# A hybrid decoder trunk on one core: half-width down-weight sums, weights read straight from the input, sums beside the stored blocks, and longer runs ahead and at the end

## The chip, the core and the metric

The kernel runs on one core of a Trainium2 chip. The core has a matrix engine (TensorE, PE in the rows), a vector engine (VectorE, DVE), a scalar engine (ScalarE, ACT), GpSimd (POOL) and a sync engine (SyncE, SP) that issues nearly all transfers here. The metric is the device time of one execution in microseconds. The three runs of the kernel before took 1681.66, 1688.73 and 1690.01 us; their median is 1688.73 us.

## The reference

One decoder layer over 1024 tokens of width 1024: two attention branches, a mixed output product, a layer norm, a SwiGLU feed-forward of inner width 2816, and a second layer norm. The change touches only the feed-forward and what follows it.

```python
proj = x @ w_in[l]
o_a = _fox_attention(...)          # forgetting attention, 8 heads of 64
o_b = _dsa_attention(...)          # indexer, top-k keys, attention with ALiBi
merged = (sigmoid(g_a) * (o_a @ w_branch_a[l]) + sigmoid(g_b) * (o_b @ w_branch_b[l]))
x = _layer_norm(ALPHA * x + merged @ w_out[l], ln1_g[l], ln1_b[l])
gate, up = jnp.split(x @ w_ffn_in[l], 2, axis=-1)
ffn = (silu(gate) * up) @ w_ffn_out[l]
x = _layer_norm(ALPHA * x + ffn, ln2_g[l], ln2_b[l])
```

## The kernel before

Every product of matrices is made from three matmuls: each operand is split into a high part, rounded by ScalarE (`split`, line 770, for the up weights; line 898 for the last product), and a low part, the difference, made by GpSimd (lines 771 and 900) or VectorE (line 899); `mm3` multiplies high by high (line 99), low by high (100) and high by low (101).

Projections and attention fill the first half of the program. Then come the branch products, the output product and the first layer norm. The feed-forward is done by a seven-product scheme over two-by-two blocks of tokens, features and columns instead of eight plain products. Its up part runs over 22 chunks c of 128 inner columns. A chunk loads its gate weights (tag `wraw`, 2 buffers) and up weights (`wup`, 2 buffers). VectorE makes four sums r1 to r4 of them (lines 818 to 821), and the seven weight blocks are split into slots of a ring (`slot`). The seven products of 12 matmuls each follow in a fixed order: the two of `c11` (weights a11, a12), then s2, s3, s1, s4 and a22. VectorE takes each product out of PSUM with one or two additions (lines 787 and 838); ScalarE applies the gate's function; lines 846 and 847 finish the two halves of h. PSUM holds eight products at a time.

The order of TensorE's work is as the program is written. The streams of the other engines are each in order, too, but a scheduler chose that order when the kernel was built: it places a VectorE instruction of one chunk ahead of or behind those of another by its own estimate of when they become ready. An engine whose next instruction must wait holds back all that stand behind it.

Two chunks (`AHEAD`) have their `c11` done before the loop, between the transposes (`turn`) of the normalised tokens; the first two chunks of the loop then start with s2.

The down part needs, for each pair j of chunks, seven sums of blocks of h and seven sums of blocks of the down weights. Both are made inside the up loop and stored to DRAM, to `abd[p][j]`, p being the product. After each odd chunk, a buffer `wb` (one buffer of 128x2048) is loaded with the down weights of the pair; three of its four blocks are stored as they are (line 859); four sums are made in place by VectorE (lines 860 to 863) and stored (line 865). The blocks of h go the same way: three are stored plain (line 868), four sums are made in place over them (lines 869 to 872), and these are stored (line 874). A sum in place must wait until the store of the block that it overwrites is done.

The last part makes the seven down products in the order p = 1, 2, 6, 5, 3, 7, 4, each over 11 pairs j, and each j over four token tiles t of 3 matmuls. `prepare(p, j)` loads one `abd[p][j]` of 512 KB and splits it. The first seven loads use the two `wraw` buffers, later ones mostly `fraw` (4 buffers). `closing(p, t)` adds a product to the output rows. The last product, p = 4, runs its first five j over all four tiles in turn and then its last six (`LASTC`) tile by tile, so that each tile's layer norm can start while the next tile is multiplied. The first norm's result is read back (`y<-ydr`) during p = 2 and p = 6, at j = 4.

Of the kernel before, what the change touches and what calls it, by code (L numbers as in the profile page):

```python
# [8 lines left out]
F32 = mybir.dt.float32  # L9
F32R = mybir.dt.float32r  # L10
# [3 lines left out]
OP = mybir.AluOpType  # L14
# [21 lines left out]
IDX_SCALE = (8 ** -0.5) * (64 ** -0.5)  # L36

NMM, NT = 2, 2
AHEAD, LASTC, HURRY = 2, 6, 100
NG = (1, 1, 2, 2, 2, 2, 2, 4)  # L40
ORDER = (3, 0, 2, 1)
PHB, PLB = 3, 3
# [7 lines left out]
def trunk_kernel(ctx: ExitStack, tc: tile.TileContext, xT, xn, wt, wbr, wout, wfi, wfo,  # L50
                 lnp, bf, alq, alk, out):
    nc = tc.nc
    te, dve, act, pool, sp = nc.tensor, nc.vector, nc.scalar, nc.gpsimd, nc.sync
# [10 lines left out]
    wp, _w = open_pool("wp")  # L64
# [3 lines left out]
    def f(ap):  # L68
        return ap.bitcast(F32)
# [60 lines left out]
    abd = [[dram.tile([128, 2, 512], F32, name=f"abd{p}_{j}") for j in range(PAIRS)] for p in range(8)]  # L130
# [37 lines left out]
    z = idx.tile([128, L], F32, name="z", tag="t4", bufs=4)  # L168
    for h in range(2):
        s = slice(h * 512, h * 512 + 512)  # L170
        ps = ps_mm()
# [22 lines left out]
    u = t4("u")  # L194
# [27 lines left out]
    r2 = [idx.tile([128, L], F32R, name=f"r2{i}", tag="t4", bufs=4) for i in range(2)]  # L222
# [18 lines left out]
    for c in range(4):  # L241
        w = split_w(raw0, pool) if c == 0 else load_w(wt[C_IQ + c])
        iq = [idx.tile([128, 768], F32R, name="iq", tag="iq", bufs=4) for _ in range(2)]
        for q, (half, c0, n, d0) in enumerate(((0, 256, 256, 0), (1, 0, 512, 256))):
            ps = ps_mm()
# [6 lines left out]
        for a in range(2):  # L252
            h = 2 * c + a
            for i in range(2, 8):
                n = 128 * (i + 1)
# [477 lines left out]
    for t in range(NB):  # L733
        half, c0 = divmod(t * 128, 512)
        bs = fin.tile([128, 2, 6], F32, name="bs", tag="bs", bufs=2)
        for n in range(2):
            ns = slice(n * 512, n * 512 + 512)
            ps = ps_b()
# [54 lines left out]
    for c in range(AHEAD):  # L793
        raw = load_raw(wfi[c])
        w = [slot(), slot()]
# [9 lines left out]
        return psC.tile([128, 512], F32, name="pb", tag="pb", bufs=8)  # L805

    ffl, _ffl = open_pool("ffl")
    ring[0:0] = [(ffl, f"wt{k}", 1) for k in range(4)]
    for c in range(FC):
        g = load_raw(wfi[c])  # L810
        up = ffl.tile([128, 1024], F32, name="wup", tag="wup", bufs=2)
        sp.dma_start(up, wfi[FC + c])
        g1_, g2_, u1_, u2_ = g[:, 0:512], g[:, 512:1024], up[:, 0:512], up[:, 512:1024]
        new = c >= len(ahead)
        a11, a12 = (slot(), slot()) if new else (None, None)
        s2, s3, s1, s4, a22 = (slot() for _ in range(5))
        r1, r2, r3, r4 = (ffl.tile([128, 512], F32, name="ss", tag="ss", bufs=4) for _ in range(4))
        dve.tensor_tensor(r1, u1_, u2_, op=OP.add)
        dve.tensor_tensor(r2, r1, g1_, op=OP.subtract)
        dve.tensor_tensor(r3, g1_, u1_, op=OP.subtract)  # L820
        dve.tensor_tensor(r4, g2_, r2, op=OP.subtract)
        if new:
            split(a11, g1_)
            split(a12, g2_)
        split(s2, r2)
        split(s3, r3)
        split(s1, r1)
        split(s4, r4)
        split(a22, u2_)
        u = c11(ps_c, (a11, a12)) if new else ahead[c]  # L830
        h = ffl.tile([128, 2, 512], F32, name="h", tag="h", bufs=3)
        U, sg, h0, h1 = u[:, 0], u[:, 1], h[:, 0], h[:, 1]

        def add(to, w, x, *more):
            ps = ps_c()
            product(ps, w, x)
            for o, i in ((to, to), *more) if to is not None else more:
                dve.tensor_tensor(o, ps, i, op=OP.add)

        add(U, s2, T2)  # L840
        add(None, s3, T3, (h0, U))
        add(None, s1, T1, (h1, h0), (U, U))
        add(U, s4, B22)
        act.activation(U, U, AF.Silu)
        add(h0, a22, T4)
        dve.tensor_tensor(h1, h1, U, op=OP.mult)
        dve.tensor_tensor(h0, h0, sg, op=OP.mult)
        if c % 2 == 0:
            even = h
            continue  # L850


        j = c // 2
        wb = ffl.tile([128, 2, 1024], F32, name="wb", tag="wb", bufs=1)
        for x in range(2):
            sp.dma_start(wb[:, x], wfo[(c - 1 + x) * 128:(c + x) * 128])
        b11, b12, b21, b22 = wb[:, 0, 0:512], wb[:, 0, 512:1024], wb[:, 1, 0:512], wb[:, 1, 512:1024]
        for p, b in ((1, b11), (2, b21), (3, b22)):
            sp.dma_start(abd[p][j][:, 1], b)
        dve.tensor_tensor(b11, b12, b11, op=OP.subtract)  # L860
        dve.tensor_tensor(b12, b22, b12, op=OP.subtract)
        dve.tensor_tensor(b22, b22, b11, op=OP.subtract)  # L862
        dve.tensor_tensor(b21, b21, b22, op=OP.subtract)  # L863
        for p, b in ((5, b11), (7, b12), (6, b22), (4, b21)):
            sp.dma_start(abd[p][j][:, 1], b)
        a11, a21, a12, a22 = even[:, 0], even[:, 1], h0, h1
        for p, a in ((1, a11), (2, a12), (4, a22)):
            sp.dma_start(abd[p][j][:, 0], a)
        dve.tensor_tensor(a22, a21, a22, op=OP.add)
        dve.tensor_tensor(a21, a11, a21, op=OP.subtract)  # L870
        dve.tensor_tensor(a11, a22, a11, op=OP.subtract)
        dve.tensor_tensor(a12, a12, a11, op=OP.subtract)
        for p, a in ((5, a22), (7, a21), (6, a11), (3, a12)):
            sp.dma_start(abd[p][j][:, 0], a)
    _ffl.close()
    _ffr.close()
# [10 lines left out]
    def prepare(p, j):  # L887
        k = len(fring)
        fring.append(None)
        if k % 2 == 0:  # L890
            big = xm.tile([128, 2, 4, 512], F32R, name="fs", tag="x", bufs=4) if k // 2 % 6 < 4 else \
                fe.tile([128, 2, 4, 512], F32R, name="fs", tag="fs", bufs=2)
            fring[k] = big
        s = fring[k - k % 2][:, k % 2]
        raw = wp.tile([128, 1024], F32, name="wraw", tag="wraw", bufs=2) if k < 7 or k % 3 == 0 else \
            fe.tile([128, 1024], F32, name="fraw", tag="fraw", bufs=4)
        sp.dma_start(raw, abd[p][j].rearrange("p a n -> p (a n)"))
        act.activation(s[:, 0:2].rearrange("p a n -> p (a n)"), raw, AF.Copy)  # L898
        dve.tensor_tensor(s[:, 2], raw[:, 0:512], f(s[:, 0]), op=OP.subtract)  # L899
        pool.tensor_tensor(s[:, 3], raw[:, 512:1024], f(s[:, 1]), op=OP.subtract)  # L900
        return s[:, 0], s[:, 2], s[:, 1], s[:, 3]
# [10 lines left out]
    def scaled(o, i):  # L912
        dve.scalar_tensor_tensor(o, o, ALPHA, i, op0=OP.mult, op1=OP.add)

    def plus(o, ps, a=None):
        dve.tensor_tensor(o, ps, o if a is None else a, op=OP.add)

    def closing(p, t, ps):

        y, z = (yt + [None] * NB)[t:t + 5:4]  # L920
        u, bs, bz = us[t], bss[t], bss[t + 4]
        if p == 1:
            act.activation(u, ps, AF.Copy)
        elif p == 2:
            scaled(y[:, ha], ps)
            plus(y[:, ha], u)
            dve.bn_stats(bs[:, 0, :], y[:, ha])
        elif p == 6:
            plus(u, ps)
        elif p == 5:  # L930
            v = fy.tile([128, 512], F32, name="v", tag="v", bufs=2)
            plus(v, ps, u)
            scaled(y[:, hb], v)
            scaled(z[:, hb], v)
        elif p == 3:
            plus(y[:, hb], ps)
            dve.bn_stats(bs[:, 1, :], y[:, hb])
            for ns in layer_norm(fy, y, bs, *V2, True):
                sp.dma_start(out[t * 128:t * 128 + 128, ns], y[:, ns])
        elif p == 7:  # L940
            plus(u, ps)
            plus(z[:, hb], ps)
            dve.bn_stats(bz[:, 1, :], z[:, hb])
            scaled(z[:, ha], u)
        else:
            plus(z[:, ha], ps)
            dve.bn_stats(bz[:, 0, :], z[:, ha])
            for ns in layer_norm(fy, z, bz, *V2, t < 2):
                sp.dma_start(out[(t + 4) * 128:(t + 5) * 128, ns], z[:, ns])

    for p in (1, 2, 6, 5, 3, 7, 4):
        acc = [psD.tile([128, 512], F32, name="acc", tag="acc", bufs=8) for _ in range(4)]
        tiles = []
        for j in range(PAIRS):
            if j == 4 and p in (2, 6):
                for t in range(4):
                    yt.append(fy.tile([128, D], F32, name=f"y{len(yt)}"))
                    sp.dma_start(yt[-1], ydr[len(yt) - 1])
            elif j == 4 and p == 5:
                V2.extend((ln_vec(fy, 2), ln_vec(fy, 3)))  # L960
            if p == 1 and j < 5:
                with tc.high_priority(offset=HURRY):
                    tiles.append(prepare(p, j))
            else:
                tiles.append(prepare(p, j))
            if p != 4 or j < PAIRS - LASTC:
                for t in range(4):
                    step(acc, t, tiles[j:], j)
        for t in range(4):
            if p == 4:  # L970
                step(acc, t, tiles[PAIRS - LASTC:], PAIRS - LASTC)
            closing(p, t, acc[t])
# [59 lines left out]
```

## Time and profile before

| | value |
|---|---|
| median of three runs | 1688.73 us |
| the profiled execution, its own time | 1686.29 us |
| its span (first to last instruction) | 1684.4 us |
| TensorE matmuls, busy | 1606.5 us (95%) |
| VectorE busy | 1160.9 us (69%) |
| ScalarE busy | 771.7 us (46%) |
| GpSimd busy | 671.3 us (40%) |
| moved by DMA | 216.18 MB, 128 GB/s on average |

TensorE is busy nearly all the time, so the time is the sum of its matmuls and of the places where it stands still or runs at its lower clock. Such places are found by asking for the busy time of stretches of the span; what ended each stop is found by asking for the waits in that stretch. The up loop runs from 1026.8 to 1457.6 us of the span, the down products from 1457.6 to 1673.1 us.

### The profile page before, as it was taken

Reading aid. Unit: us, or ns where it says so; the run is one execution under the profiler, and the core shown is the slowest. Engines: PE = TensorE matmul, PEld = TensorE weight load, DVE = VectorE, ACT = ScalarE, POOL = GpSimd, SP = SyncE. Lnnn points to the kernel's source line nnn. Section 1 sums busy time; section 2 is a strip of 40 time slices with the busy share of each in tenths; the row PEclk is TensorE's granted clock in tenths of the full one; section 3 lists DMA queues with packets and bytes.
Section 4 is the critical chain, followed back from the end, with each engine's and each line's share of the span. In section 5 each row is a group of like instructions: output and inputs, shape, how many; then the busy total and the mean of one; then the engine's idle time right before and its main releaser. Section 6 shows DMA issues by size and latency. Waiting matters only on the chain. (4 is left out here: it accounts for less than half of the span.)

```text
span 1684.4 us, 22398 instructions
## 1 busy us (share of the span) xinstructions
PE 1606.5 (95%) x7722; PEld 1312.0 (78%) x7722; DVE 1160.9 (69%) x2016; ACT 771.7 (46%) x1368; POOL 671.3 (40%) x646
## 2 busy tenths in 40 slices
PE   7898999998999999999989998999899999999997
PEld 5776887776888888888767876887778888878885
DVE  6889999979645454544466668868786665557577
ACT  6777878884444444544322024222233323254341
POOL 1122333332333333333432036444455444377673
PEclk9999999999999999999999998999999999999998
DMA  5112212121222222223886115677643332497652
GB/s 176 47 40 65 60 45 59 57 70 43 57 68 61 70 57 74 59 63 124 272 257 242 77 51 175 233 247 257 234 160 120 106 107 93 143 342 272 190 165 93
DMA packets 83817, 216.18 MB, mean 128 GB/s; under 512 B 10164, under 2 KB 14260, under 8 KB 83704
## 3 DMA queue, kind: packets, MB, share of 16 engines
q1 hardware_dynamic: 83704, 214.75, 39.0%
q8 instruction: 61, 1.00, 0.2%
q14 instruction: 52, 0.43, 0.1%
HBM read 139.93 MB, written 65.87 MB: 122 GB/s over the span
## 5 line engine op out<-in xcount | busy, mean ns | idle before, releaser
L99 PE MATMUL mm<-xh,whi 128*128 128x512 f32 (+1 forms) x720 | 296.4, 412 | 15.5 <-ACT whi L146 6.4
L101 PE MATMUL mm<-xl,whi 128*128 128x512 f32 (+1 forms) x720 | 281.9, 392 | 1.2 <-DVE xl L156 1.2
L100 PE MATMUL mm<-xh,wlo 128*128 128x512 f32 (+1 forms) x720 | 281.4, 391 | 0.5 <-DVE wlo L147 0.5
L478 POOL TENSOR_SCALAR p<-p,st 128x512 f32<-128x512 f32 (+1 forms) x192 | 113.3, 598 | 321.3 <-DVE st L475 268.6
L93 POOL TENSOR_TENSOR wlo<-wraw,whi 128x1024 fp32r<-128x1024 f32 x51 | 123.1, 2414 | 192.3 <-ACT whi L92 171.0
L771 POOL TENSOR_TENSOR w<-ss,w 128x512 fp32r<-128x512 f32 x88 | 130.4, 1496 | 165.6 <-ACT w L770 158.2
L101 PEld LDWEIGHTS mm<-xl,whi 128*128 128x128 f32 x720 | 136.1, 189 | 32.2 <-DVE xl L156 2.4
L99 PEld LDWEIGHTS mm<-xh,whi 128*128 128x128 f32 x720 | 136.9, 190 | 29.6 <-issue 6.4
L100 PEld LDWEIGHTS mm<-xh,wlo 128*128 128x128 f32 x720 | 137.3, 191 | 13.0 <-DVE wlo L147 1.0
L503 DVE TENSOR_TENSOR pl<-T,ph 128x512 fp32r<-128x512 f32 (+1 forms) x160 | 100.7, 634 | 36.6 <-ACT ph L502 34.7
L99 PE MATMUL acc<-fs 128*128 128x512 f32 x308 | 120.4, 391 | 2.8 <-ACT fs L898 2.8
L101 PE MATMUL acc<-fs 128*128 128x512 f32 x308 | 120.5, 391 | 0.6 <-POOL fs L900 0.6
L100 PE MATMUL acc<-fs 128*128 128x512 f32 x308 | 120.4, 391 | 0.2 <-DVE fs L899 0.2
L502 ACT ACTIVATE ph<-T 128x512 fp32r<-128x512 f32 (+1 forms) x160 | 87.3, 552 | 38.8 <-PE T L501 34.5
L309 ACT ACTIVATE junk<-sm,nt 128x1024 bf16<-128x1024 f32 (+2 forms) x93 | 96.8, 1040 | 14.6 <-DVE nt L317 12.8
L501 PE MATMUL T<-identf,p 128*128 128x128 f32 x576 | 90.5, 273 | 4.8 <-POOL p L478 2.5
L501 PEld LDWEIGHTS T<-identf,p 128*128 128x128 f32 x576 | 71.2, 140 | 26.8 <-POOL p L478 4.4
L900 POOL TENSOR_TENSOR fs<-fraw,fs 128x512 fp32r<-128x512 f32 x47 | 80.7, 1730 | 27.8 <-ACT fs L898 27.8
L511 PE MATMUL O<-pl,V 128*128 128x256 f32 x320 | 82.8, 282 | 1.8 <-DVE pl L503 1.8
L510 PE MATMUL O<-ph,V 128*128 128x256 f32 x320 | 83.6, 283 | 0.0
L899 DVE TENSOR_TENSOR fs<-fraw,fs 128x512 fp32r<-128x512 f32 x47 | 54.4, 1169 | 39.8 <-ACT fs L898 39.8
L771 POOL TENSOR_TENSOR w<-wraw,w 128x512 fp32r<-128x512 f32 x44 | 64.8, 1485 | 35.7 <-ACT w L770 26.9
(278 smaller groups left out, 4107.5 us busy)
## 6 DMA issues: line engine op xcount, KB each, us to landing
fraw<-abd SPq DMA_DIRECT2D x47, 512.0 KB
wraw<-in_wt_dram SPq DMA_DIRECT2D x45, 512.0 KB
abd<-wb SPq DMA_DIRECT2D x77, 256.0 KB
abd<-h SPq DMA_DIRECT2D x77, 256.0 KB
wraw<-abd SPq DMA_DIRECT2D x30, 512.0 KB
wraw<-in_wfi_dram SPq DMA_DIRECT2D x24, 512.0 KB
wup<-in_wfi_dram SPq DMA_DIRECT2D x22, 512.0 KB
wb<-in_wfo_dram SPq DMA_DIRECT2D x22, 512.0 KB
```

Of the source, the lines that this page charges most:

```text
L93: pool.tensor_tensor(lo, raw, f(hi), op=OP.subtract)
L99: te.matmul(ps, ah, bh, start=(first and i == 0), stop=False)
L100: te.matmul(ps, al, bh, start=False, stop=False)
L101: te.matmul(ps, ah, bl, start=False, stop=(last and i == n - 1))
L309: act.activation(j[:, :128 * (i + 1)], SM[i], AF.Sign, bias=bias(x), accum_out=s[:, x:x + 1])
L478: pool.tensor_scalar(pc, pc, st[:, 3:4], 1.0, op0=OP.mult, op1=OP.mult)
L501: te.transpose(T[:, s * 128:s * 128 + 128], P[qq][:, j * 128:j * 128 + 128], identf)
L502: act.activation(ph[:, c:], T[:, c:], AF.Copy)
L503: dve.tensor_tensor(pl[:, c:], T[:, c:], f(ph[:, c:]), op=OP.subtract)
L510: te.matmul(O, V[:, j, :], ph[:, r0:r0 + 256], start=(j == 0), stop=False)
L511: te.matmul(O, V[:, j, :], pl[:, r0:r0 + 256], start=False, stop=(last and jj == 1))
L771: pool.tensor_tensor(s[:, 1], raw, f(s[:, 0]), op=OP.subtract)
```

## The change

Six edits, all in the feed-forward:

- three chunks instead of two have their `c11` done before the loop, and the ring's order is changed so that the first of the loop's own slots serves the third of them;
- `wb` holds, after every chunk, half the columns of the pair's four weight blocks (128x4x256): two loads, four sums on 128x256, four stores of 128 KB each; the plain weight blocks are no longer stored;
- p = 1, 2 and 3 then load their plain weight block from the input `wfo` and their h block from `abd`, with two transfers instead of one;
- the sums q2, q3, q4 of h blocks go to tiles of the tag that r1 to r4 use (five buffers instead of four), one sum stays in place over a block that is not being stored;
- at the start of the last part the second to fifth raw loads use the free weight buffers `whi` and `wlo`, six instead of five tiles are hurried, and the read-back of the first norm's result moves from j = 4 to j = 8;
- p = 6 now finishes one scaling that p = 7 did, so p = 7 closes a tile with three VectorE instructions instead of four, and the last product runs one j over all tiles and its last ten tile by tile.

```diff
-AHEAD, LASTC, HURRY = 2, 6, 100
+AHEAD, LASTC, HURRY = 3, 10, 100
...
-    ring[0:0] = [(ffl, f"wt{k}", 1) for k in range(4)]
+    ring[0:0] = [(ffl, "wt0", 1)]
+    ring += [(ffl, f"wt{k}", 1) for k in range(1, 4)]
...
-        r1, r2, r3, r4 = (ffl.tile([128, 512], F32, name="ss", tag="ss", bufs=4) for _ in range(4))
+        r1, r2, r3, r4 = (ffl.tile([128, 512], F32, name="ss", tag="ss", bufs=5) for _ in range(4))
...
-        wb = ffl.tile([128, 2, 1024], F32, name="wb", tag="wb", bufs=1)
-        for x in range(2):
-            sp.dma_start(wb[:, x], wfo[(c - 1 + x) * 128:(c + x) * 128])
-        b11, b12, b21, b22 = wb[:, 0, 0:512], wb[:, 0, 512:1024], wb[:, 1, 0:512], wb[:, 1, 512:1024]
-        for p, b in ((1, b11), (2, b21), (3, b22)):
-            sp.dma_start(abd[p][j][:, 1], b)
+        j, x = divmod(c, 2)
+        cols = slice(x * 256, x * 256 + 256)
+        wb = ffl.tile([128, 4, 256], F32, name="wb", tag="wb", bufs=1)
+        for y in range(2):
+            rows = wfo[(2 * j + y) * 128:(2 * j + y + 1) * 128]
+            sp.dma_start(wb[:, 2 * y:2 * y + 2], rows.rearrange("p (a n) -> p a n", a=2)[:, :, cols])
+        b11, b12, b21, b22 = (wb[:, y] for y in range(4))
         dve.tensor_tensor(b11, b12, b11, op=OP.subtract)
         dve.tensor_tensor(b12, b22, b12, op=OP.subtract)
         dve.tensor_tensor(b22, b22, b11, op=OP.subtract)
         dve.tensor_tensor(b21, b21, b22, op=OP.subtract)
         for p, b in ((5, b11), (7, b12), (6, b22), (4, b21)):
-            sp.dma_start(abd[p][j][:, 1], b)
+            sp.dma_start(abd[p][j][:, 1, cols], b)
...
-        dve.tensor_tensor(a22, a21, a22, op=OP.add)
-        dve.tensor_tensor(a21, a11, a21, op=OP.subtract)
-        dve.tensor_tensor(a11, a22, a11, op=OP.subtract)
-        dve.tensor_tensor(a12, a12, a11, op=OP.subtract)
-        for p, a in ((5, a22), (7, a21), (6, a11), (3, a12)):
+        q2, q3, q4 = (ffl.tile([128, 512], F32, name="ss", tag="ss", bufs=5) for _ in range(3))
+        dve.tensor_tensor(q3, a11, a21, op=OP.subtract)
+        dve.tensor_tensor(a21, a21, a22, op=OP.add)
+        dve.tensor_tensor(q2, a21, a11, op=OP.subtract)
+        dve.tensor_tensor(q4, a12, q2, op=OP.subtract)
+        for p, a in ((7, q3), (5, a21), (6, q2), (3, q4)):
             sp.dma_start(abd[p][j][:, 0], a)
...
+        if 2 <= k < 6:
+            raw = f(wp.tile([128, 1024], F32R, name="w", tag=("whi", "wlo")[k % 2], bufs=2))
+        elif k < 7 or k % 3 == 0:
...
-        sp.dma_start(raw, abd[p][j].rearrange("p a n -> p (a n)"))
+        if p > 3:
+            sp.dma_start(raw, abd[p][j].rearrange("p a n -> p (a n)"))
+        else:
+            r0, c0 = (2 * j + (p > 1)) * 128, (p > 2) * 512
+            sp.dma_start(raw[:, 512:1024], wfo[r0:r0 + 128, c0:c0 + 512])
+            sp.dma_start(raw[:, 0:512], abd[p][j][:, 0])
...
         elif p == 6:
             plus(u, ps)
+            scaled(z[:, ha], u)
...
         elif p == 7:
-            plus(u, ps)
             plus(z[:, hb], ps)
             dve.bn_stats(bz[:, 1, :], z[:, hb])
-            scaled(z[:, ha], u)
+            plus(z[:, ha], ps)
...
-            if j == 4 and p in (2, 6):
+            if j == 8 and p in (2, 6):
...
-            if p == 1 and j < 5:
+            if p == 1 and j < 6:
```

VectorE's stream at the end of chunk 1, before. The row with `h<-pb,h` takes the chunk's last product out of PSUM; lines 818 to 821 are r1 to r4, lines 869 to 872 the sums of h blocks.

```order
L838 TENSOR_TENSOR u<-pb,u 128x512 x2
L846 TENSOR_TENSOR h<-h,u 128x512
L838 TENSOR_TENSOR h<-pb,h 128x512
L847 TENSOR_TENSOR h<-h,u 128x512
L818 TENSOR_TENSOR ss<-wup 128x512
L869 TENSOR_TENSOR h<-h 128x512
L870 TENSOR_TENSOR h<-h 128x512
L871 TENSOR_TENSOR h<-h 128x512
L819 TENSOR_TENSOR ss<-ss,wraw 128x512
```

The same place after. Lines 819 and 820 are now r1 and r2, lines 873 to 875 the sums of h blocks, 858 to 861 the weight sums.

```order
L873 TENSOR_TENSOR h<-h 128x512
L839 TENSOR_TENSOR h<-pb,h 128x512
L874 TENSOR_TENSOR ss<-h 128x512
L848 TENSOR_TENSOR h<-h,u 128x512
L859 TENSOR_TENSOR wb<-wb 128x256
L875 TENSOR_TENSOR ss<-h,ss 128x512
L819 TENSOR_TENSOR ss<-wup 128x512
L860 TENSOR_TENSOR wb<-wb 128x256
L820 TENSOR_TENSOR ss<-ss,wraw 128x512
```

The r1 and r2 behind the last product are those of chunk 4 in the stream before, and those of chunk 2, the very next one, in the stream after.

VectorE's stream between the last two down products, before: the closings of p = 7 on its last two tiles, then the low part (line 899) of the eleventh tile of p = 4, then the first closing of p = 4.

```order
L916 TENSOR_TENSOR us_13343<-acc,us_13343 128x512
L916 TENSOR_TENSOR y_13848<-acc,y_13848 128x512
L913 SCALAR_TENSOR_TENSOR y_13848<-y_13848,us_13343 128x512
L943 BN_STATS bs_13351<-y_13848 128x6
L916 TENSOR_TENSOR us_13344<-acc,us_13344 128x512
L916 TENSOR_TENSOR y_13850<-acc,y_13850 128x512
L913 SCALAR_TENSOR_TENSOR y_13850<-y_13850,us_13344 128x512
L943 BN_STATS bs_13352<-y_13850 128x6
L899 TENSOR_TENSOR fs<-fraw,fs 128x512
L916 TENSOR_TENSOR y_13844<-acc,y_13844 128x512
```

The same place after, with all four tiles of p = 7 (line 911 is the low part).

```order
L911 TENSOR_TENSOR fs<-wraw,fs 128x512
L928 TENSOR_TENSOR y_14059<-acc,y_14059 128x512 x2
L955 BN_STATS bs_13472<-y_14059 128x6
L928 TENSOR_TENSOR y_14061<-acc,y_14061 128x512 x2
L955 BN_STATS bs_13473<-y_14061 128x6
L928 TENSOR_TENSOR y_14063<-acc,y_14063 128x512 x2
L955 BN_STATS bs_13474<-y_14063 128x6
L928 TENSOR_TENSOR y_14065<-acc,y_14065 128x512 x2
L955 BN_STATS bs_13475<-y_14065 128x6
L911 TENSOR_TENSOR fs<-fraw,fs 128x512
L928 TENSOR_TENSOR y_14059<-acc,y_14059 128x512
```

The closings are twelve instructions instead of sixteen; the eleventh tile's low part still stands behind all of them.

## Rows read from the trace of the kernel before

**Rows 1.** Stretches: length, busy us (instructions) of PE, PEld, DVE, ACT, POOL; PEclk; DMA.

```profile
1021.56:1033.81 12.25, 5.15 (x11) 3.76 (x12) 11.80 (x12) 6.49 (x12) 9.06 (x6) 0.59 0.35 111
1036.00:1233.00 197.00, 189.15 (x813) 152.43 (x812) 153.20 (x181) 48.82 (x90) 102.13 (x69) 1.00 0.70 240
1230.00:1240.00 10.00, 8.45 (x30) 6.88 (x31) 9.02 (x13) 2.68 (x5) 3.34 (x3) 0.83 0.71 235
1240.00:1457.60 217.60, 217.60 (x944) 176.99 (x943) 139.00 (x173) 67.55 (x111) 108.59 (x77) 1.00 0.31 102
1470.00:1490.00 20.00, 16.32 (x64) 12.66 (x63) 8.51 (x8) 7.41 (x7) 11.63 (x8) 0.91 0.85 305
1500.00:1640.00 140.00, 140.00 (x619) 115.94 (x618) 99.10 (x118) 60.29 (x65) 99.91 (x61) 1.00 0.67 224
1670.00:1680.00 10.00, 3.11 (x14) 2.25 (x12) 9.58 (x21) 1.72 (x4) 2.99 (x2) 0.78 0.28 106
```

**Rows 2.** What PE waited for, 1021 to 1034: total us, times, longest.

```profile
PE pb L99 <- ACT w L770: 5.2, 1, 5.2
PE pb L100 <- POOL w L771: 1.9, 1, 1.9
```

**Rows 3.** What PE waited for, 1160 to 1240.

```profile
PE pb L99 <- DVE h L838: 3.9, 2, 2.6
PE pb L99 <- DVE u L838: 3.4, 2, 2.7
```

**Rows 4.** What DVE waited for, 1036 to 1233.

```profile
DVE wb L860 <- issue: 9.7, 2, 5.7
DVE wb L860 <- DMA abd<-wb: 5.8, 2, 3.5
...
DVE h L869 <- DMA abd<-h: 5.1, 3, 2.3
```

**Rows 5.** The chain in order of time near 1215: start, length, what.

```profile
1213.26 3.84 DMA abd<-wb
1217.25 4.75 DMA wb<-in_wfo_dram
```

**Rows 6.** Issues of line 865: count, ns min/median/max, first to last start.

```profile
L865 SPq DMA_DIRECT2D abd<-wb x44: 319/320/578, 1036.8 to 1232.6; - x44
```

**Rows 7.** Groups by shape, 1027 to 1457: count, busy us, mean ns, idle before.

```profile
L771 POOL TENSOR_TENSOR w<-ss,w 128x512 fp32r<-128x512 f32 x88 | 130.4, 1496 | 165.6 <-ACT w L770 158.2 <-DVE h L838 7.5
...
L770 ACT ACTIVATE w<-ss 128x512 fp32r<-128x512 f32 x86 | 52.5, 624 | 40.4 <-PE pb L101 35.7 <-DVE ss L821 2.1 <-DVE ss L820 1.1
...
L838 DVE TENSOR_TENSOR h<-pb,h 128x512 f32<-128x512 f32 x43 | 29.6, 688 | 13.3 <-PE pb L101 12.3
```

**Rows 8.** Timeline near 1023: a GpSimd split begun alone (start, length).

```profile
1023.46 1.26 POOL L771 TENSOR_TENSOR w<-wup,w 128x512 fp32r<-128x512 f32 x1 [28.08 <-ACT w L770]
```

**Rows 9.** Groups by shape, whole span: a VectorE operation on 128x256.

```profile
L431 DVE TENSOR_TENSOR V<-mm,V 128x256 fp32r<-128x256 f32 x32 | 13.3, 417 | 3.5 <-ACT V L430 3.0
```

**Rows 10.** Timeline 1470 to 1480: start, length, instruction, [idle before, releaser].

```profile
1470.54 0.58 SPq L958 DMA_DIRECT2D y<-ydr  x1
...
1471.17 12.36 SPq L897 DMA_DIRECT2D fraw<-abd  x6
...
1479.69 0.49 PE L99 MATMUL acc<-fs 128*128 128x512 f32 x1 [2.82 <-ACT fs L898]
```

**Rows 11.** Timeline of DVE from 1646 to 1660: the closings of p = 7.

```profile
1647.41 1.29 DVE L899 TENSOR_TENSOR fs<-wraw,fs 128x512 fp32r<-128x512 f32 x1 [0.42 <-ACT fs L898]
1648.62 0.68 DVE L916 TENSOR_TENSOR us<-acc,us 128x512 f32<-128x512 f32 x1
...
1658.19 0.67 DVE L899 TENSOR_TENSOR fs<-fraw,fs 128x512 fp32r<-128x512 f32 x1
```

**Rows 12.** Timeline of DVE at the end: p = 4, tiles 2 and 3.

```profile
1669.68 0.69 DVE L916 TENSOR_TENSOR y<-acc,y 128x512 f32<-128x512 f32 x1
...
1676.02 0.69 DVE L916 TENSOR_TENSOR y<-acc,y 128x512 f32<-128x512 f32 x1
```

More of the change, by code (lines that the diff above doesn't have):

```diff
@@ L847, in trunk_kernel @@
         dve.tensor_tensor(h0, h0, sg, op=OP.mult)
[L848 to L853, printed above, removed]
-        wb = ffl.tile([128, 2, 1024], F32, name="wb", tag="wb", bufs=1)
-        for x in range(2):
-            sp.dma_start(wb[:, x], wfo[(c - 1 + x) * 128:(c + x) * 128])
-        b11, b12, b21, b22 = wb[:, 0, 0:512], wb[:, 0, 512:1024], wb[:, 1, 0:512], wb[:, 1, 512:1024]
-        for p, b in ((1, b11), (2, b21), (3, b22)):
-            sp.dma_start(abd[p][j][:, 1], b)
+        j, x = divmod(c, 2)
[5 more added lines that the diff above has]
+        b11, b12, b21, b22 = (wb[:, y] for y in range(4))
         dve.tensor_tensor(b11, b12, b11, op=OP.subtract)
@@ L864, in trunk_kernel @@
         for p, b in ((5, b11), (7, b12), (6, b22), (4, b21)):
-            sp.dma_start(abd[p][j][:, 1], b)
+            sp.dma_start(abd[p][j][:, 1, cols], b)
+        if x == 0:
+            even = h
+            continue
         a11, a21, a12, a22 = even[:, 0], even[:, 1], h0, h1
@@ L894, in prepare @@
         s = fring[k - k % 2][:, k % 2]
-        raw = wp.tile([128, 1024], F32, name="wraw", tag="wraw", bufs=2) if k < 7 or k % 3 == 0 else \
-            fe.tile([128, 1024], F32, name="fraw", tag="fraw", bufs=4)
-        sp.dma_start(raw, abd[p][j].rearrange("p a n -> p (a n)"))
+        if 2 <= k < 6:
+            raw = f(wp.tile([128, 1024], F32R, name="w", tag=("whi", "wlo")[k % 2], bufs=2))
+        elif k < 7 or k % 3 == 0:
+            raw = wp.tile([128, 1024], F32, name="wraw", tag="wraw", bufs=2)
+        else:
+            raw = fe.tile([128, 1024], F32, name="fraw", tag="fraw", bufs=4)
+        if p > 3:
+            sp.dma_start(raw, abd[p][j].rearrange("p a n -> p (a n)"))
+        else:
+            r0, c0 = (2 * j + (p > 1)) * 128, (p > 2) * 512
+            sp.dma_start(raw[:, 512:1024], wfo[r0:r0 + 128, c0:c0 + 512])
+            sp.dma_start(raw[:, 0:512], abd[p][j][:, 0])
         act.activation(s[:, 0:2].rearrange("p a n -> p (a n)"), raw, AF.Copy)
```

## Prediction, on record before the changed kernel ran

> **What bounds the kernel now.** TensorE is busy for 95% of the span, so I looked first for the stretches where it isn't, by a table of busy time in slices of 10 us, then asked in each such stretch what TensorE waited for, then what the engine it waited for had waited for itself. A stretch in which TensorE is held by nothing gives the pace: 619 matmuls in 140 us or 0.226 us each among the down products, and 944 in 217.6 us or 0.23 in the up loop, so a product of 12 takes 2.8 us and a chunk of 84 takes 19.4 us [rows 1]. Four places lose time against that pace.
>
> The border between the early chunks and the loop: 12.25 us hold 11 matmuls, which are worth 2.5 us, so 9.7 us are lost [rows 1]. Of these 5.2 and 1.9 us are waits for the high and low part of the first weight block [rows 2]; the rest is the granted clock of 0.59 there.
>
> The loop from 1160 to 1240: waits of 3.9, 3.4 and (the difference to the idle time) 0.6 us for VectorE to empty PSUM [rows 3]; 189.15 us busy of 197 say the same, 7.9 us idle [rows 1]. From 1230 to 1240 the clock was 0.83, and 30 matmuls (6.9 us) took 8.45: 1.6 us more. Together 9.4 us. VectorE was late because it stood in its own order before the weight sums and the sums over stored blocks: 5.8 us for stores of `wb`, 5.1 us for stores of h, 9.7 us on what the trace calls issue [rows 4]. Eleven pairs took from 1036.8 to 1232.6, 17.9 us each [rows 6], and after that the loop loses nothing: 217.6 us busy of 217.6 [rows 1].
>
> The start of the down products: 64 matmuls in 20 us are 14.5 us of work, so 5.5 us are lost [rows 1], 2.8 of them one wait for a tile whose load went out at 1471.2, behind the read-back of the first norm's result [rows 10].
>
> The end: TensorE stops at 1673.1 [rows 1], but VectorE starts the last closing only at 1676.0, since that of the tile before runs from 1669.7 [rows 12]: 2.9 us.
>
> **What the change takes away.** The border: the third chunk's 24 early matmuls (5.5 us) now stand in the gap. The first loop weight's low part is there 1.9 + 5.2 us and one matmul, some 7.9 us, after the transposes end, so about 2.4 us of wait stay, and with part of the slow clock 3 (0 to 5): gain 6.7. The loop: the plain stores go, and no sum overwrites a block that is being stored, so both named waits go; the whole 9.4 us is the gain that I take, and what the new sums cost is counted below. The start of the down products: four raw loads more can be out before the first is consumed, and the read-back stands behind the loads that were late: gain 5.5 (2.8 if the slow clock comes anyway). The end: with ten pairs tile by tile, a tile's run is 30 matmuls or 6.8 us instead of 18 or 4.1, longer than the 6.3 us of the closing beside it [rows 12], so nothing is queued before the last closing: gain 2.9. Sum: 24.5 us. The scaling moved from p = 7 to p = 6 removes four VectorE operations from a place named below; p = 6's closings run under TensorE's 30 us per product, as they did.
>
> **What it adds.** First, chunk 2. In the order of VectorE, r1 and r2 of chunk 2 stand behind the last product of chunk 1 and behind the sums of h blocks that need it. Before, they stood two chunks ahead. Chunk 2 now starts with the product that needs r2, since its `c11` is already done, and nothing covers the wait. From the last matmul on: the eviction 0.69 [rows 7], then q2, the multiplication, q4 and r1 at 0.60 each (sixteen operations between 1648.62 and 1658.19 start 0.598 apart, the pace of VectorE alone [rows 11]) and a half-width weight sum at 0.4 by the nearest row of that width [rows 9], so r1 is there after 3.5 us; ScalarE's high part 0.62 [rows 7] makes 4.1. GpSimd's order is the low parts of s1, a22 and then s2, three at 1.26 alone to 1.50 on average [rows 7, 8]: 7.9 to 8.6. I take 8.2 us of idle. At the border the slow clock cost 2.6 us after such a wait; I take 2. Sum 10.2; the low end is 7.9 with no slow clock, the high end 13, if the weight sum in that row waits out the rest of a 4.75 us load [rows 5]. Nothing can make it a gain: r2 can't start before the product ends.
>
> Second, the even chunks 4 to 20, nine of them. There the same chain stands behind the odd chunk's last product, with r1 and r2 at its end: 0.69, five at 0.60 and (to chunk 10 or so) 0.4 make r2 at 4.1 and its high part at 4.7. If GpSimd takes r2 first the low part is there at 6.0 to 6.2; where it takes r1 first, as the stream does in some of them, at up to 6.9. The two products of `c11` cover 5.5 us. The wait is 0.5 to 1.4 us each, 4.5 to 12.6 in all, zero if the engines answer a little faster. I take 8.
>
> Third, the weight sums themselves. One buffer is loaded, summed, stored and loaded again, now 22 times at half the width; the stream runs them ahead of need, some two rounds per chunk until chunk 11. By the rows a load takes 4.75 us and the wait for the last store 3.84 [rows 5]; with 1.6 us for four half-width sums a round is 10.2 us, and two rounds per 19.4 us chunk would be 1.0 us late per chunk, 11 us over eleven chunks. If load and store shrink with their bytes (a half and a half), the round is some 6 us and costs nothing. VectorE's stream has nearly three rounds in an odd chunk and one in an even one, and what it is late at the end of an odd chunk, TensorE pays at the next border, where no buffer stands between them. I take 3, nearer to the short end, since the rows were taken at 240 GB/s and 0.70 of the DMA engines [rows 1] and the change moves fewer bytes.
>
> The Trainium skill, "DMA: Bandwidth & Descriptors", "Anatomy of one DMA — SWDGE (gpsimd) path", gives a transfer as about 2.0 us plus its bytes at 436 GB/s, for another issuing path than SP's. By that rule halving the stores saves little each, and a round is an estimated 2.0 + 1.2 for the load, as much for the stores, and the 1.6 for the sums, 8.0 us: no lateness, and a sum 3 us lower. The rows stand above the rule (4.75 against 3.2), so I keep the 3.
>
> Fourth, the last product. Its first pass now has one j. TensorE ends at 1673.1, and 132 matmuls before that, at 1643.3, p = 4 starts; after 12 matmuls (2.7 us) tile 0 runs through nine pairs in 6.1 us and needs the eleventh's low part at 1652.3. That low part stands on VectorE behind the closings of p = 7: these begin at 1648.62, when the tenth is done [rows 11], and twelve at 0.598 end at 1655.8; with 0.67 it is there at 1656.5. TensorE waits 4.2 us, and at the lower clock after it, as at the start of the down products (16.32 busy for 14.5 [rows 1]), loses another 1.7: 5.9 us (4.2 to 7). Before, the eleventh was needed 17 us into the product.
>
> Sum of what is added: 10.2 + 8 + 3 + 5.9 = 27.1. Against 24.5 it leaves +2.6 us on the profiled execution's own 1686.29 (a span of 1684.4 and 1.9 around it), so 1688.9. That execution is 2.4 us under the median of the runs, 1688.73, and I leave the sum where it is: **1689 us**, no change that can be told: half a per cent, 8.4 us, is what can be.
>
> **The rivals.** *The new waits are short* (faster). The chains run at VectorE's and GpSimd's lone pace, the weight rounds are never late, and short waits don't bring the clock down: the even chunks cost 4.5 instead of 8, the weight rounds 0 instead of 3, the clocks behind chunk 2 and in p = 4 give back 3.7, and the border closes wholly, 3: 13 us less, 1676 us. For it: from 1036 to 1233 the mean granted clock was 1.00 in spite of 7.9 us of waits [rows 1]. Against it: GpSimd's mean is 1.50, not 1.26 [rows 7, 8].
>
> *The weight sums hold VectorE at the end of odd chunks* (slower). The round takes the 10.2 us of the rows, and three of them in an odd chunk are waited out by TensorE at the borders to chunks 4 to 12; the even chunks cost 12.6. That is 8 more there, 4.6 more, and 3 more at chunk 2: 1704 us. It decides from a round of about 9.7 us on, half a chunk. For it: the waits of 9.7 and 5.8 us [rows 4]; against it: fewer bytes.
>
> *The loop's loss stays although the stores go*, because VectorE is late by its load and not by its waits: then 7 of the 9.4 us come back and 1696 us is the time. Against it: after 1240 the same work without `wb` loses nothing [rows 1].
>
> **How the numbers follow.** My forecast has 0.36 (1681 to 1697), the first rival 0.32, the second 0.25, the third 0.07. Faster by over 0.5%, under 1680.3: nearly all of the first, some of mine: 0.35. Slower, over 1697.2: the second, half of the third: 0.29. Same: 0.36. The range reaches into both rivals, 1671 to 1706; the ends of the unknown costs (0 to 11 for the rounds, 0 to 12.6 for the even chunks) make it so wide.
>
> **What would show it.** In the trace after: no waits of TensorE on evictions between 1160 and 1240; one wait of about 8 us at the start of chunk 2, ended by GpSimd's split (line 771); nine waits of about 1 us, one chunk in two; no gap at the start of the down products; one wait of about 4 us on VectorE's low part (line 911) some 9 us into p = 4; the last closing starting right behind the last matmul. If the wait at chunk 2 is under 4 us, my reading of VectorE's order is wrong; if waits of 3 us and more stand at chunks 4 to 12, the second rival holds.

## The result, and the profile after

The changed kernel took 1736.64 us (median of five runs, 1734.95 to 1740.23), the kernel before 1687.24 us beside it: the ratio is 1.030 (95% interval 1.028 to 1.032). It is slower by some 49 us; the forecast of no change was wrong, and the time lies outside the range. The profiled execution has a span of 1733.8 us.

Three stretches hold all of the difference but 1.2 us, which lie ahead of them. In the table by stretch (length, busy us and matmuls of PE, then the other engines, the granted clock, DMA), the up loop with its border, from the last early transpose to the first down product, is first of the kernel before, then of the changed one; both hold the same 1800 matmuls:

```profile
1021.56:1457.63 436.07, 421.12 (x1801) 340.50 (x1802) 312.24 (x373) 126.69 (x219) 225.31 (x154) 0.98 0.50 168
```

```profile
1022.80:1508.61 485.81, 434.89 (x1800) 347.42 (x1800) 320.99 (x419) 133.99 (x219) 226.82 (x153) 0.94 0.42 138
1508.61:1725.60 216.99, 211.74 (x925) 174.54 (x923) 150.23 (x187) 86.58 (x97) 139.04 (x85) 0.98 0.62 215
```

The loop is 49.7 us longer: TensorE's idle time rose from 15.0 to 50.9 us, and its busy time by 13.8 us for the same matmuls, at a mean granted clock of 0.94 against 0.98. The down products are 1.5 us longer than the 215.5 of before, and what follows TensorE's last matmul is 8.2 us instead of 11.3.

What TensorE waited for, 1020 to 1480 and 1480 to 1734 (total us, times, longest), where before it waited for evictions [rows 3]:

```profile
PE pb L99 <- ACT w L770: 28.1, 5, 9.7
PE pb L100 <- POOL w L771: 22.8, 11, 3.7
```

```profile
PE acc L100 <- DVE fs L911: 5.2, 1, 5.2
```

It now waits for the high and low parts of weights: 2.7 us at the border and 48.2 at the starts of the even chunks, nowhere else in the loop; no wait for an eviction is left. What VectorE waited for, 1020 to 1480, against [rows 4]:

```profile
DVE wb L858 <- DMA wb<-in_wfo_dram: 48.2, 17, 5.9
...
DVE wb L859 <- DMA wb<-in_wfo_dram: 12.2, 16, 2.4
```

The waits for stores are gone, as forecast, and 60 us of waits for loads have come. The start of chunk 2 shows how both meet (start, length, instruction, [idle before, releaser]):

```profile
1063.85 0.43 DVE L858 TENSOR_TENSOR wb<-wb 128x256 f32<-128x256 f32 x1 [2.14 <-DMA wb<-in_wfo_dram]
1064.19 0.69 DVE L873 TENSOR_TENSOR h<-h 128x512 f32<-128x512 f32 x1
1064.79 0.69 DVE L839 TENSOR_TENSOR h<-pb,h 128x512 f32<-128x512 f32 x1
...
1067.53 0.69 DVE L819 TENSOR_TENSOR ss<-wup 128x512 f32<-128x512 f32 x1
...
1068.47 0.69 DVE L820 TENSOR_TENSOR ss<-ss,wraw 128x512 f32<-128x512 f32 x1
...
1068.96 2.53 POOL L771 TENSOR_TENSOR w<-ss,w 128x512 fp32r<-128x512 f32 x1 [14.85 <-ACT w L770]
...
1071.45 1.26 POOL L771 TENSOR_TENSOR w<-wup,w 128x512 fp32r<-128x512 f32 x1
1071.52 1.73 DVE L819 TENSOR_TENSOR ss<-wup 128x512 f32<-128x512 f32 x1 [1.16 <-POOL w L771]
```

```profile
1069.98 0.80 PE L99 MATMUL pb<-t2h,w 128*128 128x512 f32 x1 [9.67 <-ACT w L770]
1074.43 0.80 PE L100 MATMUL pb<-t2h,w 128*128 128x512 f32 x1 [3.66 <-POOL w L771]
```

TensorE had stopped at 1060.3. VectorE takes its last product out only at 1064.8: it is late from waits before, and a weight sum (line 858) ahead of the eviction waits 2.1 us more for a load. Then come the sums, r1, r2, and three splits on GpSimd, the third of them r2's. From the eviction to the second matmul it is the predicted chain, 9.6 us long with the first matmul's 0.8 in it (8.2 of idle forecast); the 4.5 us before it are VectorE's lateness.

In the last product, the eleventh tile's low part (line 911) ends at 1702.6, and the last closing starts with no other ahead of it:

```profile
1702.64 0.80 PE L100 MATMUL acc<-fs 128*128 128x512 f32 x1 [5.25 <-DVE fs L911]
```

```profile
1725.67 0.69 DVE L928 TENSOR_TENSOR y<-acc,y 128x512 f32<-128x512 f32 x1 [1.66 <-PE acc L101]
```

### The profile page after: what moved, and what is told of

Read it like the earlier page. It is cut to its first block, busy times and chain, and to the rows that moved or that the text cites. A ratio compares the mean times of both kernels' runs of the same rounds, so it can differ in the third digit from the quotient of the medians.

```text
span 1733.8 us, 22407 instructions
## 1 busy us (share of the span) xinstructions
PE 1620.2 (93%) x7722; PEld 1319.3 (76%) x7722; DVE 1169.0 (67%) x2060; ACT 779.0 (45%) x1368; POOL 674.2 (39%) x646
## 5 line engine op out<-in xcount | busy, mean ns | idle before, releaser
L771 POOL TENSOR_TENSOR w<-ss,w 128x512 fp32r<-128x512 f32 x88 | 136.2, 1577 | 110.9 <-ACT w L770 110.9
L771 POOL TENSOR_TENSOR w<-wraw,w 128x512 fp32r<-128x512 f32 x44 | 61.2, 1397 | 103.9 <-ACT w L770 102.3
L770 ACT ACTIVATE w<-ss 128x512 fp32r<-128x512 f32 x88 | 53.6, 628 | 87.5 <-DVE ss L819 27.3
```

Source lines behind the costliest of these rows:

```text
L771: pool.tensor_tensor(s[:, 1], raw, f(s[:, 0]), op=OP.subtract)
```

## The experiments

The theory after the result: TensorE pays at the even chunks because r1 and r2 stand behind q4 on VectorE (A, the place in the stream), and VectorE is late there because its weight rounds follow one another at once (B, the rounds). All ratios are to the kernel before, with 95% intervals.

**The sums of h blocks behind r1 to r4 of the next chunk.** The block that stores and sums a pair's h becomes a function, `pair_sums`, which is called one iteration later:

```diff
         dve.tensor_tensor(r4, g2_, r2, op=OP.subtract)
+        pair_sums()
...
-        a11, a21, a12, a22 = even[:, 0], even[:, 1], h0, h1
...
+        late_sums.append((j, even, h))
```

> The sums of h blocks of a pair are written (and take their buffers) after r1 to r4 of the next chunk instead of before them; nothing else differs from the changed kernel. Theory A (place in VectorE's stream): the 48 us that TensorE waits at the starts of chunks 2 to 20 come from r1 and r2 of the even chunks standing right behind q4; with them a chunk earlier these waits go, the slow clock behind them too, and the time falls by 45 to 60 us, to 1677 to 1692 us. Theory B (weight rounds): VectorE is late by its 60 us of waits for the weight loads wherever r1 and r2 stand; then TensorE waits for evictions in place of the weights, and the time stays above 1705 us.

Measured: 1712.45 us, ratio 1.015 (1.012 to 1.017), 24 us less than the changed kernel. The waits for weights went, but for the one at the border; in their place TensorE waits for evictions, and VectorE still for loads:

```profile
PE pb L99 <- DVE u L857: 19.9, 11, 3.0
PE pb L99 <- DVE u L787: 6.0, 3, 2.5
PE pb L99 <- DVE h L857: 3.5, 6, 1.0
PE pb L100 <- POOL w L771: 2.7, 1, 2.7
```

```profile
DVE wb L876 <- DMA wb<-in_wfo_dram: 47.8, 13, 4.6
```

B's forecast came true as it stands (evictions, above 1705), but 24 us went, which B leaves out, where A had 45 to 60: neither theory alone. The place in the stream is worth about half, and the lateness of VectorE now shows as waits for evictions.

**Two chunks ahead.** `AHEAD` is 2, with the ring's order of before:

```diff
-AHEAD, LASTC, HURRY = 3, 10, 100
+AHEAD, LASTC, HURRY = 2, 10, 100
-    ring[0:0] = [(ffl, "wt0", 1)]
-    ring += [(ffl, f"wt{k}", 1) for k in range(1, 4)]
+    ring[0:0] = [(ffl, f"wt{k}", 1) for k in range(4)]
```

> The changed kernel with two chunks ahead instead of three, and the ring's order of before. Theory A: chunk 2 has its two covering products again, so its 13.3 us of wait fall to about those of chunk 4 (4 us), and the slow clock behind it (3 us) goes; the border before the loop loses 5 to 6 us more again; the waits at chunks 4 to 20 stay. Time 1725 to 1733 us. Theory B: no change at chunk 2, time 1740 us with the border's loss.

Measured: 1740.33 us, ratio 1.032 (1.029 to 1.034): a miss of both, nearer to B's number. Chunk 2's wait did fall, to 7.1 us, but not to 4, since its two covering products (5.5 us) cover only part of a chain that VectorE's lateness makes longer; the border lost its 7.1 us again. The third chunk ahead is not what makes the change slow.

**No weight sums.** The sums and their loads are left out, so what is stored are not the layer's weight sums; one buffer is loaded once and stored from:

```diff
+    wb = ffl.tile([128, 4, 256], F32, name="wb", tag="wb", bufs=1)
+    for y in range(2):
+        sp.dma_start(wb[:, 2 * y:2 * y + 2], wfo[y * 128:y * 128 + 128].rearrange("p (a n) -> p a n", a=2)[:, :, 0:256])
     for c in range(FC):
...
-        dve.tensor_tensor(b11, b12, b11, op=OP.subtract)
-        dve.tensor_tensor(b12, b22, b12, op=OP.subtract)
-        dve.tensor_tensor(b22, b22, b11, op=OP.subtract)
-        dve.tensor_tensor(b21, b21, b22, op=OP.subtract)
```

> The weight sums are left out: one buffer is loaded once before the loop and stored from, four stores per chunk as in the changed kernel; VectorE has no weight sums and no weight loads to wait for. The order of r1 and r2 behind q4 stays. Theory A with B as its size: chunk 2 still waits 7 to 9 us, chunks 4 to 20 only the chain itself, 0.5 to 2.5 us each, 24 us in all instead of 48, and the time falls to 1695 to 1708 us. Theory A alone (the chain itself is that long): 1730 us and more. Theory B alone (all is the weight loads): the waits go, 1685 us.

Measured: 1704.51 us, ratio 1.010 (1.008 to 1.013), as A with B as its size has it. TensorE stops at 1059.45 at the end of chunk 1, and VectorE begins the eviction at 1059.48: it is on time. Chunk 2 waits 8.4 us (5.08 and 3.36), the nine even chunks after it 17.2 us, 1.2 to 3.7 each. In this kernel, 1075 to 1480:

```profile
PE pb L100 <- POOL w L771: 17.2, 9, 3.7
```

So the chain by itself costs 25.6 us of waits in the loop, and the rounds add 22.6 to make the changed kernel's 48.2, with the slower clock behind them: 32 us of time.

**The last six tile by tile.** `LASTC` is 6, nothing else differs.

```diff
-AHEAD, LASTC, HURRY = 3, 10, 100
+AHEAD, LASTC, HURRY = 3, 6, 100
```

> The changed kernel with the last six instead of the last ten j tile by tile in the last product. The wait of 5.3 us for the eleventh tile's low part goes with about 1.7 us of slow clock; the last closing is late by about 3 us again. Time 1732 to 1734 us. A rival reading, that the wait would come anyway (loads late): 1738 us or more.

Measured: 1734.49 us, ratio 1.027 (1.024 to 1.031). No wait is left after 1520. TensorE ends at 1722.4, but the last closing starts at 1725.3, 2.9 us late again. This profiled execution waited 57.1 us for weights in the loop, 6 us more than that of the changed kernel, which has the same loop, and the two kernels' own runs overlap (1728.78 to 1735.71 here, 1734.95 to 1740.23 there), so the trace says more than the time.

**Rounds that can't run ahead.** Three differences: the deferred sums of the first experiment, `LASTC` 8, and

```diff
-        up = ffl.tile([128, 1024], F32, name="wup", tag="wup", bufs=2)
+        up = ffl.tile([128, 1024], F32, name="wup", tag="wup", bufs=3)
...
-        wb = ffl.tile([128, 4, 256], F32, name="wb", tag="wb", bufs=1)
+        wb = ffl.tile([128, 1024], F32, name="wb", tag="wup", bufs=3).rearrange("p (a n) -> p a n", a=4)
```

> The changed kernel with three differences: the sums of h blocks written after r1 to r4 of the next chunk, as in the first experiment; the half-width weight buffer taken from the ring of the up weights (three buffers in all, the same space), so that the rounds can't run ahead and one round stands in each chunk, with its load out a chunk earlier; the last eight j tile by tile. Theory (TensorE pays for VectorE's place in its order, and VectorE for rounds that follow each other at once): VectorE no longer waits for weight loads, TensorE no longer for weights nor for evictions between 1040 and 1490, and the wait in p = 4 falls under 1 us: 1668 to 1680 us, faster than the kernel before. Rival (the rounds cost VectorE's time wherever they stand): the 29 us of waits for evictions of the first experiment stay, 1700 us or more.

Measured: 1665.36 us, ratio 0.988 (0.986 to 0.990): faster than both kernels. TensorE's waits, 1020 to 1520, and VectorE's, 1020 to 1480:

```profile
PE pb L100 <- POOL w L771: 2.7, 1, 2.7
PE pb L99 <- DVE u L857: 1.1, 1, 1.1
```

```profile
DVE wb L876 <- DMA wb<-in_wfo_dram: 39.0, 19, 4.3
...
DVE wb L877 <- DMA wb<-in_wfo_dram: 7.9, 19, 1.4
```

The theory said that VectorE would no longer wait for loads; it waits 47 us still. What changed is that these waits come about one to a chunk, 4.3 us at most, where the first experiment had 13 for 47.8 us. Between VectorE and TensorE stand eight products in PSUM and weights split a chunk ahead, and TensorE waits 1.1 us for VectorE. In p = 4, 1.0 us of wait is left.

**Full-width rounds.** The second experiment with one round of the whole width for each pair:

```diff
-        cols = slice(x * 256, x * 256 + 256)
-        wb = ffl.tile([128, 4, 256], F32, name="wb", tag="wb", bufs=1)
...
+        wb = ffl.tile([128, 2, 1024], F32, name="wb", tag="wb", bufs=1)
         for y in range(2):
+            sp.dma_start(wb[:, y], wfo[(2 * j + y) * 128:(2 * j + y + 1) * 128])
...
-            sp.dma_start(abd[p][j][:, 1, cols], b)
+            sp.dma_start(abd[p][j][:, 1], b)
```

> The kernel of the second experiment (two chunks ahead) with full-width weight rounds: one load of a pair, four sums of 128x512, four stores, eleven rounds instead of 22; the plain blocks are still not stored. Theory that the fixed part of each load and store makes the half-width rounds dear: VectorE's 53 us of waits for weight loads fall to 20 to 30 us, TensorE's waits at the even chunks to 6 by about 10 us less, time 1715 to 1728 us. Rival (bytes count, not rounds): 1735 us or more.

Measured: 1727.96 us, ratio 1.025 (1.023 to 1.026), 12 us below its half-width partner (1740.33). VectorE's waits, 1020 to 1480:

```profile
DVE wb L859 <- DMA wb<-in_wfo_dram: 26.7, 7, 4.7
...
DVE wb L860 <- DMA wb<-in_wfo_dram: 5.0, 5, 1.4
```

Half as many rounds, and 31.7 us of waits for loads against 54.7 in the partner: per round 2.9 and 2.5 us, so the wait hardly shrank with the bytes. The time is in the theory's range; the waits are a little above its 20 to 30 us.

**The last part alone.** The kernel before with the edits of the last part, but `LASTC` 8:

```diff
-AHEAD, LASTC, HURRY = 2, 6, 100
+AHEAD, LASTC, HURRY = 2, 8, 100
...
+        if 2 <= k < 6:
+            raw = f(wp.tile([128, 1024], F32R, name="w", tag=("whi", "wlo")[k % 2], bufs=2))
...
-            if j == 4 and p in (2, 6):
+            if j == 8 and p in (2, 6):
...
-            if p == 1 and j < 5:
+            if p == 1 and j < 6:
```

> The kernel before with the change's edits of the last part alone: six raw buffers at its start, six hurried tiles, the read-back at j = 8, the scaling in p = 6, and the last eight j tile by tile (not ten, so that the eleventh tile's low part isn't late). The loop and the weight stores are as before. Expected from the predicted gains: the 5.5 us at the start of the down products and most of the 2.9 us at the end go, 1678 to 1681 us. Rival (those losses were hidden elsewhere or come back): 1685 to 1689 us.

Measured: 1687.9 us, ratio 1.001 (0.999 to 1.002): the rival. At the start of the down products TensorE still waits, 1455 to 1490:

```profile
PE acc L99 <- ACT fs L902: 3.5, 1, 3.5
PE acc L100 <- DVE fs L903: 0.6, 1, 0.6
PE acc L101 <- POOL fs L904: 0.3, 1, 0.3
```

More raw buffers don't cure that place. In the changed kernel it has no wait, so the cure is an edit of the loop that this kernel hasn't; the nearest is that the last pair's sums no longer wait for stores of h, after which the loads stand on SyncE. That edit was not tried alone. The end did gain here: 8.4 us follow TensorE's last matmul instead of 11.3. But the down products took 219.2 us against 215.5, with waits of 4.4 us at the start, a granted clock of 0.68 from 1480 to 1490 (0.83 before) and a wait of 1.4 us in p = 4, so nothing is left of that gain.

**The paced rounds alone**, without the deferred sums, and `LASTC` 10 (the second diff of the fifth experiment and nothing else).

> The changed kernel with one difference: the half-width weight buffer is taken from the ring of the up weights, as in the fifth experiment; r1 and r2 of the even chunks stay behind q4, and the last ten j go tile by tile. In VectorE's stream the odd chunks then hold no weight sums, the even ones two rounds. Theory (lateness of VectorE from the rounds adds to the chain at the even chunks): VectorE is on time at the end of an odd chunk, so chunk 2 waits 8 us and chunks 4 to 20 the chain alone, about 1.9 us each, as without the weight sums; time 1702 to 1712 us. Rival (any weight round in the loop costs the same): 1725 us or more.

Measured: 1709.58 us, ratio 1.013 (1.011 to 1.014). Chunk 2 waits 12.0 us (8.57 and 3.38), the nine others 17.3 us, 1.2 to 3.7 each: the same as without any weight sums. The theory's time came out, and the rival's didn't; for chunk 2 the expected 8 us were too few.

**Both, with the last ten tile by tile** (the fifth experiment with `LASTC` 10).

> The fifth experiment with the last ten j tile by tile, as in the changed kernel. The eleventh tile's low part stands behind twelve closings again: TensorE waits 4 to 5.5 us in p = 4 and runs at the lower clock after it, 1670 to 1673 us against 1665. Rival (the wait in p = 4 came from late loads that the other edits have cured): 1664 to 1667 us.

Measured: 1672.33 us, ratio 0.991 (0.989 to 0.993). In p = 4, after 1520:

```profile
PE acc L100 <- DVE fs L922: 5.5, 1, 5.5
```

The wait is there again with the loop cured, so it comes from the order of VectorE; it costs 7 us against the fifth experiment.

The four kernels with `LASTC` 10 make a table: changed 1736.6, sums deferred 1712.5, rounds paced 1709.6, both 1672.3 us. The two edits give 24 and 27 us alone and 64 together, more than their sum: one takes r1 and r2 away from the place where TensorE feels VectorE's lateness at once, the other keeps that lateness out of the odd chunks, and either is half of the cure.

## Why the prediction was wrong

**The step that failed** is the third term of what the change adds, the weight rounds, taken at 3 us. They cost 32 us: the changed kernel against the one without weight sums. The prediction had the mechanism as its second rival, with its place, and gave it 0.25; by its own sign, waits of 3 us and more at chunks 4 to 12, the rival holds (4.3, 7.6, 5.2, 7.3 and 3.7, of which only the last stands without weight sums too). The rival's price of 1704 us was too low as well, since it counted one microsecond per chunk of lateness and 3 at chunk 2, and no slow clock behind the waits at the even chunks.

Two steps made the term small. The sum chose between rows of 4.75 and 3.84 us [rows 5] and their halves, and went nearer to the halves because "the change moves fewer bytes". The full-width pair of kernels speaks against that: with half the bytes per round and twice the rounds, the waits for loads rose from 31.7 to 54.7 us. And it spread the rounds evenly, two to a chunk, which put the point of decision at a round of 9.7 us. The rounds bunch: VectorE's stream holds nearly three in an odd chunk, as the prediction itself says. The issues of the changed kernel's weight loads in one odd chunk:

```profile
1186.87 1.21 SPq L856 DMA_DIRECT2D wb<-in_wfo_dram  x2
1194.84 1.21 SPq L856 DMA_DIRECT2D wb<-in_wfo_dram  x2
1203.09 1.21 SPq L856 DMA_DIRECT2D wb<-in_wfo_dram  x2
```

In four such groups of three the rounds follow one another at 7.8 to 9.9 us, 8.5 on average. That is under 9.7, but three of them are an estimated 25.5 us in a chunk of 19.4, some 6 us late at its end; three fit only from 6.5 us down. TensorE waited 4.9 us more at chunk 2 than without the sums, and 4.4 more at each of chunks 4 to 10. With the rounds paced, no weight sum stands in an odd chunk, and the waits at the even chunks after chunk 2 are those without any sums (17.3 and 17.2 us).

From the Trainium skill, "DMA: Bandwidth & Descriptors", section "Anatomy of one DMA — SWDGE (gpsimd) path", the prediction had only an estimated round of 8.0 us. The section says there that a transfer has a fixed part of about 2 us, which doesn't scale with its bytes, for another issuing path than SP's. The estimate is near the 8.5 us of the trace; the "no lateness" that was drawn from it does not follow, since three such rounds stand in one chunk.

**Chunk 2** was right in its chain: 8.2 us forecast, 8.4 without weight sums. In the changed kernel it is 13.3, by the high end of 13 and by the kind of cause that was named for it: a weight sum that waits for its load, only ahead of the eviction and not behind it.

**The even chunks** were forecast at 0.5 to 1.4 us each, 8 in all. Without the rounds they are 1.2 to 3.7, 17.2 in all: a size that was off by two, and one reason why the kernel without weight sums is still 18 us above the kernel before, where the sum without its third term comes out at nothing; the rest of the 18 was not taken apart. The low part of r2 was taken at GpSimd's 1.26 to 1.50 us, and beside VectorE's sums one split took 2.53 us at chunk 2, and 1.77 in the kernel without weight sums; the order that puts r1's split first adds another. With the rounds chunks 4 to 10 wait 24.4 us instead of 6.8 (of 34.8 in all nine).

**The slow clock** was credited 2 us behind chunk 2 and 1.7 in p = 4. TensorE's busy time for the same matmuls rose by 13.8 us in the loop, since waits of 4 to 13 us now come five times over (chunks 2 to 10), each with slices at a clock of 0.51 to 0.85 about it; the slice behind the 3.7 us of chunk 12 is at 0.83, and the waits of 1.2 to 2.3 us of chunks 14 to 20 left it at 1.00. Two slices of 10 us of the changed kernel, at chunk 8 and at chunk 16 (columns as above):

```profile
1210.00:1220.00 10.00, 5.03 (x11) 3.66 (x12) 9.30 (x12) 4.49 (x8) 5.89 (x4) 0.58 0.60 206
...
1390.00:1400.00 10.00, 7.75 (x34) 5.96 (x33) 10.00 (x9) 5.52 (x10) 9.73 (x6) 1.00 0.41 125
```

The first holds 11 matmuls in 5.03 us of busy time, 0.46 each; the second 34 in 7.75, 0.23 each: the first lies mostly at the lower of TensorE's two levels (1.2 and 2.4 GHz), the second at the upper one.

**The gains** came nearly as forecast. The waits for evictions at 1160 to 1240 are gone, and VectorE no longer waits for stores. But the changed kernel alone doesn't show that gain, since TensorE's stops at the even chunks let VectorE catch up: with those stops taken away in the first experiment, 29.4 us of waits for evictions stood in the loop, and only the paced rounds brought them to 1.1. The border keeps 2.7 us of wait (2.4 forecast). The start of the down products has no wait (5.5 gained), but not by the raw buffers alone, to which the prediction gave it: with them and the loop of before, 4.4 us of wait stood there. The end gained 3.1 us (2.9 forecast), with VectorE free 1.7 us before the last closing.

**The last product** waits 5.25 us (4.2 forecast; the forecast's own terms, 1643.3 + 2.7 + 6.1, give 1652.1 and not 1652.3, so 4.4). The paced pair prices it at 7 us with its clock, against 5.9 forecast. Another sum is off without consequence: 195.8 us over eleven pairs are 17.8 each, not 17.9.

## What to carry to other kernels

Before giving sums to a ring of buffers that other sums use, look at which of them then stand behind which in the engine's order, and whether those were what ran ahead. Here r1 and r2 came to stand right behind q4 when q2, q3 and q4 joined their ring, and writing the sums in the other order undid it; no run changed the ring alone, so that it is the ring which ties them is not shown. Judge an in-order engine's waits by what stands next in its stream and by what buffers lie between it and the bottleneck, not by their sum: here 60 us of VectorE's waits came with 51 us of TensorE's in the changed kernel, and 47 us with 3.8 in the paced one. Splitting a load, sum and store round in two to save space doubles the number of trips, and should be counted in trips; and where the trips bunch, count them in the fullest stretch, not on average.

## What the runs showed of the hardware

A half-width VectorE sum (128x256) took 0.43 us at chunk 2, where GpSimd did nothing, but up to 0.70 us on average over the loop:

```profile
L860 DVE TENSOR_TENSOR wb<-wb 128x256 f32<-128x256 f32 x22 | 15.3, 697 | 0.5
```

In the rows of chunk 2, a GpSimd split begun beside VectorE's sums (1068.96) took 2.53 us, and those sums 0.69 each; the next split (1071.45) took 1.26 us, as one begun alone did [rows 8], and the VectorE sum that began just after it 1.73. So an overlap didn't lengthen both alike there, now the one and now the other; by what, no run here took apart.
